# A blocked triangular inverse inside an RWKV-7 scan: rank-1 updates kept to 16x16 diagonal blocks, the block below them by fp32 products on TensorE

## The chip, the cores and the metric

The kernel runs on one core of one Trainium2 chip. The metric is device time in microseconds (us) of one execution. The engines are called as the profile calls them: PE (TensorE, matrix products; PEld is its weight load), DVE (VectorE), ACT (ScalarE), POOL (GpSimd) and SP (SyncE, which issues the DMAs).

## The reference, cut to what matters

Two groups of 512 tokens go through two layers: RWKV-7 time mixing (layer 0) and neighbourhood attention (layer 1). The change touches layer 0 alone, where for 16 heads of width 64, in both directions, this recurrence is computed:

```python
def step(s, inp):
    r_t, w_t, k_t, v_t, a_t, b_t = inp
    sa = jnp.einsum('bhvk,bhk->bhv', s, a_t)
    s = s * w_t[:, :, None, :] + sa[..., None] * b_t[:, :, None, :] + v_t[..., None] * k_t[:, :, None, :]
    return s, jnp.einsum('bhvk,bhk->bhv', s, r_t)
```

## The kernel before

**Chunks.** The scan is worked in chunks of 64 tokens, eight for each sequence. Inside a chunk the terms `sa` of the 64 tokens depend on each other through a strictly lower triangular matrix of scalar products ("gram"), so each chunk needs the inverse of a unit triangular 64x64 matrix for each head and direction. The work goes in eight sets: two sequences `s`, and for each four pairs of head pairs `pb`. A set has 4 heads, 2 directions and 8 chunks, which makes 64 matrices of 64x64; they lie in two halves of the partitions as 32 units.

**Stages of a set.** `prep` (called twice for a set by `preps`) builds decays and the four scaled operands `ab`, and `gram` multiplies them (L951) and copies the 32x32 diagonal blocks into `Gd` (L957) and the blocks below them into `Go` (L958). `inverse` turns these into `MT`, the transposed inverses. Then eight `step`s run, one for each chunk and direction pair: each solves with `MT` (L1189), forms outputs (L1213) and the next state `S` (L1209, L1221, L1223). `finish` normalises what the eight steps left.

**The inverse.** For each of 128 partitions, `N` holds one 32x32 diagonal block in its rows, so that 128 blocks are worked at once. Thirty rank-1 updates, each a product (L994) and a sum (L996) over the rows below, invert the block. A mask (L998) and a diagonal of ones (L1000) follow, then two transposes of 32x32 blocks (L1004 into `NA`, L1009 into `MT`). ACT and POOL spread `MT` (L1013, L1014), and PE multiplies twice with 32x32 tiles (L1025, L1027) to get the block below the two diagonal blocks of the 64x64 matrix, with copies by ACT in between (L1032, L1035).

**What else runs in the same phase.** The dense products of the layer ("columns") run in the background: 80 columns of 128 outputs, each 8 trios of 128x128 by 128x512 products in a split fp32 form (L802, L803, L804), 640 trios in all. Their weights are split into a high and a low part by ACT (L721) and DVE (L723), their inputs likewise (L747, L749).

**What sets the order.** All of this is written as threads (`step`, `alone`, `near`, `outer`, `preps`, `inverse`, `finish`, the parts of `flow`), and `weave` decides at build time, with the estimated durations in `Clock`, in which order their pieces are put on PE, DVE and ACT. The order on the chip is fixed: each engine takes its instructions one after the other, and one that waits holds up all behind it. A thread has a rank; `step` has 0, `preps` 1.5, `inverse` 5, the columns 9, and lower goes first. Where nothing can run on PE for a while in its estimates, `weave` puts in filler products whose results nobody reads (L1622). `MT` has two buffers, so the inverse of a set waits for the steps of the set two before it. `Gd` has one buffer, so the second half of the gate in `preps` (`did["gd"] >= n`) holds back the preparation of a set until the inverse before it has taken its copy.

```python
yield "S", lambda: did["gd"] >= n and did["inverse"] >= n - 1      # preps
yield "D", lambda: did["preps"] > n and did["steps"] >= NCH * (n - 1)   # inverse
Thread(lambda: 5, inverse()), Thread(lambda: 1.5, preps())
```

After the scan phase `rest` runs the remaining columns of layer 0, and layer 1.

## Time and profile before

| | |
|---|---|
| median of 3 runs | 1686.07 us (1684.14 to 1687.42) |
| the profiled execution | 1683.88 us, of it the span of the trace 1682.1 us |
| mean granted TensorE clock | 0.971 of full speed |
| busy, share of the span: PE, PEld, DVE, ACT, POOL | 93%, 71%, 73%, 58%, 1% |
| first solve of the eight steps of a set (L1189), us from the start | 321, 443, 558, 664, 790, 920, 1041, 1115 |
| last step of the scan (L1213) | 1162 |
| last trio of the background columns in this phase | 1179 |

The profile is of one execution. All times in it count from the start of the span. A row of the timeline has a start, a duration, the engine, the line and the operation, with output and inputs by the program's names; rows of a table by stretch have the stretch, its length, and for each engine the busy time and the number of instructions in it. An fp32 product has two records in the trace, so 512 products of a line show as x1024.

### The profile page before, as it was taken

What the parts mean: (1) busy time and instruction counts of PE and PEld (TensorE: products, weight loads), DVE (VectorE), ACT (ScalarE), POOL (GpSimd) and SP (SyncE); (2) the same over time, 40 slices, a digit from 0 to 9 for tenths busy, and PEclk for the clock granted to TensorE, in tenths of its full rate; (3) what the DMA queues carried; (4) which work ended last, traced back from release to release, by engine and by line L of the source; (5) the groups of instructions that cost most, each with busy time, mean ns of one, the idle gap of its engine ahead of it and who ended that gap; (6) DMA issues with size and microseconds to landing.
All of it is one profiled execution on the core that took longest, in us unless ns stands there. A gap on an engine that the chain in (4) does not pass through costs nothing.

```text
span 1682.1 us, 46291 instructions
## 1 busy us (share of the span) xinstructions
PE 1570.9 (93%) x18818; PEld 1201.2 (71%) x18818; DVE 1227.8 (73%) x2725; ACT 984.0 (58%) x1977; POOL 24.1 (1%) x94
## 2 busy tenths in 40 slices
PE   7989898899989998989998999999999899999998
PEld 6767666676766776767765767777777687777776
DVE  8985668688777697887888887865576856555564
ACT  5443655676655667755674665454577655555562
POOL 0000000000000000000000000000000000000000
PEclk9989999899999999999997999999999999999999
DMA  5435678678586786876776665554774347555553
GB/s 209 163 125 187 203 243 261 202 228 257 170 262 211 225 255 205 259 243 205 241 232 214 202 199 199 184 178 131 267 231 155 111 127 249 182 157 175 164 181 107
DMA packets 240821, 336.26 MB, mean 200 GB/s; under 512 B 53696, under 2 KB 119360, under 8 KB 240608
## 3 DMA queue, kind: packets, MB, share of 16 engines
q1 hardware_dynamic: 240608, 333.31, 61.6%
q8 instruction: 148, 2.42, 0.6%
q14 instruction: 65, 0.53, 0.1%
HBM read 227.71 MB, written 105.51 MB: 198 GB/s over the span
## 4 chain that ended last, share of the span: by engine, by line
PE 67%; DVE 11%; DMA 9%; ACT 8%; issue 4%; SPq 1%; DVEq 0%; POOL 0%; ACTq 0%; POOLq 0%
PE pm L802 7%; PE pg L423 6%; PE pg L424 6%; PE pg L425 6%; PE pm L804 5%; PE pm L803 5%; PE pf L1090 2%; PE sc L1433 2%; PE us L1209 2%; DMA cab<-dab 2%; PE po L1466 2%; PE pt L1451 2%; PE zy L1162 2%; PE us L1189 2%; PE zy L1213 1%
## 5 line engine op out<-in xcount | busy, mean ns | idle before, releaser
L802 PE MATMUL pm<-act,whi 128*128 128x512 f32 x640 | 287.6, 449 | 16.1 <-ACT act L771 7.2
L804 PE MATMUL pm<-act,wlo 128*128 128x512 f32 x640 | 256.7, 401 | 12.2 <-DVE wlo L723 12.2
L803 PE MATMUL pm<-act,whi 128*128 128x512 f32 x640 | 258.0, 403 | 5.1 <-DVE act L749 4.2
L423 PE MATMUL pg<-act,whi 128*128 128x512 f32 x448 | 182.4, 408 | 5.9 <-ACT act L372 5.5
L424 PE MATMUL pg<-act,whi 128*128 128x512 f32 x448 | 178.1, 398 | 0.1
L425 PE MATMUL pg<-act,wlo 128*128 128x512 f32 x448 | 177.5, 396 | 0.0
L802 PEld LDWEIGHTS pm<-act,whi 128*128 128x128 f32 x640 | 122.6, 192 | 63.8 <-issue 16.1
L372 ACT CAST whi<-raw 128x512 fp32r<-128x512 f32 x148 | 91.4, 619 | 129.3 <-PE pg L424 75.3
L804 PEld LDWEIGHTS pm<-act,wlo 128*128 128x128 f32 x640 | 123.4, 193 | 44.3 <-DVE wlo L723 16.9
L373 DVE TENSOR_TENSOR wlo<-raw,whi 128x512 fp32r<-128x512 f32 x148 | 101.4, 687 | 70.2 <-ACT whi L372 63.0
L803 PEld LDWEIGHTS pm<-act,whi 128*128 128x128 f32 x640 | 123.6, 193 | 29.6 <-DVE act L749 7.2
L723 DVE TENSOR_TENSOR wlo<-raw,whi 128x512 fp32r<-128x512 f32 x160 | 108.7, 684 | 42.9 <-ACT whi L721 39.5
L721 ACT CAST whi<-raw 128x512 fp32r<-128x512 f32 x160 | 98.1, 616 | 51.7 <-PE pm L803 14.5
L423 PEld LDWEIGHTS pg<-act,whi 128*128 128x128 f32 x448 | 84.8, 190 | 24.8 <-ACT act L372 6.1
L425 PEld LDWEIGHTS pg<-act,wlo 128*128 128x128 f32 x448 | 84.8, 189 | 17.9 <-issue 0.8
L424 PEld LDWEIGHTS pg<-act,whi 128*128 128x128 f32 x448 | 84.9, 190 | 17.4 <-issue 2.0
L996 DVE TENSOR_TENSOR N<-etmp,N 128x30 f32<-128x30 f32 (+14 forms) x240 | 78.5, 327 | 4.2
L994 DVE TENSOR_TENSOR etmp<-N 128x30 f32<-128x30 f32 (+14 forms) x240 | 78.3, 326 | 4.2
L1444 DVE CUSTOM_DVE_ANT_0 sb<-sc,bias 128x256 f32<-128x256 f32 x128 | 49.2, 419 | 31.1 <-PE pt L1451 23.5
L1090 PE MATMUL pf<-cab 64*64 64x128 f32 (+1 forms) x2048 | 67.9, 268 | 2.2 <-issue 2.1
L1447 ACT ACTIVATE sb<-sb,mx 128x256 f32<-128x256 f32 x128 | 63.9, 504 | 9.1 <-DVE mx L1446 9.0
L1113 DVE TENSOR_TENSOR AK<-zy,cc 128x256 f32<-128x256 f32 x63 | 26.6, 421 | 53.5 <-PE zy L1068 51.6
(389 smaller groups left out, 3389.7 us busy)
## 6 DMA issues: line engine op xcount, KB each, us to landing
dab<-ab SPq DMA_DIRECT2D x32, 1024.0 KB, 5.5
cab<-dab SPq DMA_DIRECT2D x64, 512.0 KB, 4.4
raw<-in_w_in_dram SPq DMA_DIRECT2D x128, 256.0 KB, 3.3
bias<-in_rpb_dram SPq DMA_DIRECT2D x32, 384.0 KB, 4.8
raw<-in_w_z_dram SPq DMA_DIRECT2D x32, 256.0 KB, 4.5
dz<-tmp SPq DMA_DIRECT2D x32, 256.0 KB, 3.0
raw<-in_w_k_dram SPq DMA_DIRECT2D x32, 256.0 KB, 4.0
dk<-tmp SPq DMA_DIRECT2D x32, 256.0 KB, 2.2
```

Source lines behind the costliest of these rows:

```text
L372: self.nc.scalar.copy(hi, src)
L373: (eng or self.nc.vector).tensor_tensor(lo, src, hi.bitcast(F32), op=ALU.subtract)
L423: nc.tensor.matmul(ps, hi, x[k][0], start=(k == 0), stop=False)
L424: nc.tensor.matmul(ps, hi, x[k][1], start=False, stop=False)
L425: nc.tensor.matmul(ps, lo, x[k][0], start=False, stop=(k == KT - 1))
L721: nc.scalar.copy(hi, raw[h])
L723: nc.vector.tensor_tensor(lo, raw.pop(h), hi.bitcast(F32), op=ALU.subtract)
L802: nc.tensor.matmul(ps, hi[:, at], xh, start=(k == 0), stop=False)
L803: nc.tensor.matmul(ps, hi[:, at], xl, start=False, stop=False)
L804: nc.tensor.matmul(ps, lo[:, at], xh, start=False, stop=(k == KT - 1))
L996: vt.tensor_tensor(N[:, q + 1:, :q], tv, N[:, q + 1:, :q], op=ALU.add)
L1090: end = nc.tensor.matmul(st.f[half(a), h, 0, d, g] if st.last else st.f[half(a), h, :, d, g], ab[half(h), d, g, 2 * e[d] + 1 - a], rt if s ...
```

## The change

The rank-1 updates now work only inside the two 16x16 blocks on the diagonal of each 32x32 block: 14 updates instead of 30, with both 16x16 blocks in one instruction (a leading dimension of 2 in the access pattern `blocks`). The two 16x16 blocks off the diagonal of `N` are zeroed by a memset on POOL. The mask covers 512 elements in place of 1024. Both transposes now write into `MT`, and the tile `NA` is gone; `N` is used again in its place.

The 16x16 block below the two diagonal blocks is then made by three rounds of fp32 products on PE (`each`): 32 units, four positions of the PE array (rows and columns 0, 32, 64, 96), 128 products of 32x32 by 32x16 in a round, all into one PSUM tile. Between the rounds DVE evacuates once (a scaling by a 0/1 column and an added identity) and ACT twice. A round waits for the evacuation before it. What follows, the 64x64 step with L1025 and L1027, stays, reading `MT` and `N` in place of `NA`.

`Gd` gets a second buffer, and the gate `did["gd"] >= n` is dropped from `preps`. Two small constants are made once at the start. Line numbers behind the change are higher by 3 to 29.

```diff
+        self.i32 = cp.tile([P, 33], F32, tag="i32", name="i32")
+        nc.vector.tensor_reduce(self.i32[:, 0:32], self.ident.rearrange("p (q m) -> p m q", q=4), axis=AX.X, op=ALU.add)
+        nc.vector.tensor_reduce(self.i32[:, 32:33], self.i32[:, 16:32], axis=AX.X, op=ALU.add)
...
-                self.t("wc", (P, 2, 2, NCH), 4, F32, self.front), self.t("Gd", (P, 2, NCH, 2, 32), 1, F32, self.front),
+                self.t("wc", (P, 2, 2, NCH), 4, F32, self.front), self.t("Gd", (P, 2, NCH, 2, 32), 2, F32, self.front),
...
-        tmp = f("etmp", (P, 256))
-        self.did["gd"] += 1
-        for q in range(1, 31):
-            n = 31 - q
-            tv = tmp[:, :n * q].rearrange("p (i j) -> p i j", i=n)
+        tmp = f("etmp", (P, 128))
+
+        def blocks(o, i, j):
+            x = N[:, 0, 0:1]
+            return bass.AP(tensor=x.tensor, offset=x.offset + o, ap=[list(x.ap[0]), [16 * 33, 2], list(i), list(j)])
+
+        x = N[:, 0, 16:17]
+        gps.memset(bass.AP(tensor=x.tensor, offset=x.offset, ap=[list(x.ap[0]), [16 * 31, 2], [32, 16], [1, 16]]), 0.0)
+        for q in range(1, 15):
+            n = 15 - q
+            tv = tmp[:, :2 * n * q].rearrange("p (b i j) -> p b i j", b=2, i=n)
+            here = blocks(32 * (q + 1), (32, n), (1, q))
             yield "D"
-            vt.tensor_tensor(tv, N[:, q + 1:, q:q + 1].broadcast_to([P, n, q]), N[:, q:q + 1, :q].broadcast_to([P, n, q]), op=ALU.mult)
+            vt.tensor_tensor(tv, blocks(32 * (q + 1) + q, (32, n), (0, q)), blocks(32 * q, (0, n), (1, q)), op=ALU.mult)
             yield "D"
-            vt.tensor_tensor(N[:, q + 1:, :q], tv, N[:, q + 1:, :q], op=ALU.add)
+            vt.tensor_tensor(here, tv, here, op=ALU.add)
         yield "D"
-        vt.tensor_tensor(N, N, self.lower, op=ALU.mult)
+        here = blocks(0, (32, 16), (1, 16))
+        vt.tensor_tensor(here, here, self.lower[:, 0:16, 0:16].unsqueeze(1).broadcast_to([P, 2, 16, 16]), op=ALU.mult)
...
-        NA = f("NA", (P, NU, 32))
-        vt.transpose(NA.rearrange("p u j -> p j u"), N.rearrange("p i j -> p j i"))
+        vt.transpose(MT[:, :, 1, :].rearrange("p u j -> p j u"), N.rearrange("p i j -> p j i"))
         yield "D"
         vt.transpose(MT[:, :, 0, :].rearrange("p u i -> p i u"), N)
         yield "A"
+        act.copy(N[:, :, 16:32], self.i32[:, 16:32].unsqueeze(1).broadcast_to([P, NU, 16]))
+        quarters = [slice(32 * q, 32 * q + 32) for q in range(4)]
+
+        def each(lhs, rhs, *xs):
+            yield "P", free, lambda c: max(room(c), need(*xs)(c))
+            ps = self.p("pm", (P, NU, 16))
+            for u in range(NU):
+                for q in quarters:
+                    nc.tensor.matmul(ps[q, u], lhs(q, u), rhs(q, u), start=True, stop=True, tile_position=(q.start, q.start))
+            return ps
+
+        ps = yield from each(lambda q, u: gd[q, u], lambda q, u: MT[q, u, 1, 0:16], MT, Gd)
+        yield "D", None, need(ps)
+        vt.scalar_tensor_tensor(
+            N[:, :, 0:16], ps, self.i32[:, 32:33], self.i32[:, 0:16].unsqueeze(1).broadcast_to([P, NU, 16]), op0=ALU.mult, op1=ALU.add)
+        ps = yield from each(lambda q, u: MT[q, u, 0], lambda q, u: N[q, u, 0:16], MT, N)
+        yield "A", None, need(ps)
+        act.copy(MT[:, :, 1, 0:16], ps)
+        ps = yield from each(lambda q, u: N[q, u], lambda q, u: MT[q, u, 0, 16:32], MT, N)
+        yield "A", None, need(ps)
+        act.copy(MT[:, :, 0, 16:32], ps)
+        yield "A"
...
-                            nc.tensor.matmul(ps[y, j], go[x, u], NA[x, u], start=True, stop=True, tile_position=(64 * h, 64 * h + 32))
+                            nc.tensor.matmul(ps[y, j], go[x, u], MT[x, u, 1], start=True, stop=True, tile_position=(64 * h, 64 * h + 32))
...
-                yield "S", lambda: did["gd"] >= n and did["inverse"] >= n - 1
+                yield "S", lambda: did["inverse"] >= n - 1
```

**What moves on PE.** Of the 640 trios of the columns, those that stand ahead of the first solve of the last set are 596 before and 428 now; the rest, 44 before and 212 now, stand behind it. The filler products (L1622) are 97 before and 70 now. On PE, around the products of the second set's inverse, before (names ending in numbers are buffers; "x31" stands for 31 more of the same):

```order
L802 MATMUL pm_5001<-act_4070,whi_4940 128x512
L803 MATMUL pm_5001<-act_4069,whi_4940 128x512
L804 MATMUL pm_5001<-act_4070,wlo_4941 128x512
L1025 MATMUL pm_5030<-NA_4982,Go_2466 32x32 [waits DVE_49,Activation_49]
L1025 MATMUL pm_5030<-NA_4982,Go_2466 32x32 x31
L802 MATMUL pm_5001<-act_4113,whi_4970 128x512
```

and the rounds of the same inverse in the change (the first and the second, with what stands between them):

```order
L1028 MATMUL pm_4474<-MT_440_1700,Gd_2468 32x16 x128
L1191 MATMUL zy_4627<-S_4470,cab_441_1701 64x64 [waits DVE_49]
L1191 MATMUL zy_4627<-S_4470,cab_441_1701 64x64 x15
L1197 MATMUL zy_4627<-V_4239,AK_4439 64x64 [waits DMAHW5_49]
L1197 MATMUL zy_4627<-V_4239,AK_4439 64x64 x7
L954 MATMUL pf_4656<-ab_4211 32x64 [waits Activation_49]
L954 MATMUL pf_4656<-ab_4211 32x64 x31
L683 MATMUL pm_4691<-cc,tmp_4383 128x128 x4
L1028 MATMUL pm_4701<-N_3818,MT_440_1700 32x16 [waits DVE_49]
L1028 MATMUL pm_4701<-N_3818,MT_440_1700 32x16 x63
```

Before, trios of columns stand on both sides of the inverse's products; in the change, products of a step (L1191, L1197) and of a gram (L954) of the sets around it stand between two rounds.

On DVE, the end of the second set's updates in the change (L1250 and L1252 make the state of a step of the first set, L1142 and L1152 its factors):

```order
L1004 TENSOR_TENSOR etmp_3820<-N_3818 128x28 [waits DVE_49]
L1152 TENSOR_TENSOR R_4314<-pf_4285,mrx_1696 128x512 [waits PE_49]
L919 TENSOR_TENSOR ab_4211<-kp_873_4306,u_4208 128x4x2x64 [waits DVE_49]
L1250 TENSOR_TENSOR S_4334<-us_4268,S_4180 128x256 [waits PE_49,Activation_49]
L1006 TENSOR_TENSOR N_3818<-etmp_3820,N_3818 128x2x14 [waits DVE_49]
L1252 TENSOR_TENSOR S_4334<-S_4334,wc_1785 128x256 [waits DVE_49]
L1259 TENSOR_TENSOR y_3124<-zy_4214,y_3124 128x256 [waits PE_49]
L1009 TENSOR_TENSOR N_3818<-N_3818,cc 128x2x16x16 [waits DVE_49]
L1011 MEMSET N_3818 128x32 [waits DVE_49,Pool_49]
```

Before, the last update of the second set stands behind the last step of the first set and its `finish`; in the change it stands among the steps of the first set, as the states `S` show.

More of the change, by code (lines that the diff above doesn't have):

```diff
@@ L987, in inverse @@
         vt.transpose(N, gd.rearrange("p u t -> p t u"))
-        tmp = f("etmp", (P, 256))
-        self.did["gd"] += 1
-        for q in range(1, 31):
-            n = 31 - q
-            tv = tmp[:, :n * q].rearrange("p (i j) -> p i j", i=n)
+        tmp = f("etmp", (P, 128))
[8 more added lines that the diff above has]
+            here = blocks(32 * (q + 1), (32, n), (1, q))
             yield "D"
-            vt.tensor_tensor(tv, N[:, q + 1:, q:q + 1].broadcast_to([P, n, q]), N[:, q:q + 1, :q].broadcast_to([P, n, q]), op=ALU.mult)
+            vt.tensor_tensor(tv, blocks(32 * (q + 1) + q, (32, n), (0, q)), blocks(32 * q, (0, n), (1, q)), op=ALU.mult)
             yield "D"
-            vt.tensor_tensor(N[:, q + 1:, :q], tv, N[:, q + 1:, :q], op=ALU.add)
+            vt.tensor_tensor(here, tv, here, op=ALU.add)
         yield "D"
-        vt.tensor_tensor(N, N, self.lower, op=ALU.mult)
+        here = blocks(0, (32, 16), (1, 16))
+        vt.tensor_tensor(here, here, self.lower[:, 0:16, 0:16].unsqueeze(1).broadcast_to([P, 2, 16, 16]), op=ALU.mult)
         yield "D"
         vt.memset(N.rearrange("p i j -> p (i j)")[:, 0:1024:33], 1.0)
-        yield "D"
-        NA = f("NA", (P, NU, 32))
-        vt.transpose(NA.rearrange("p u j -> p j u"), N.rearrange("p i j -> p j i"))
         MT = self.MTb[self.nM % 2]
@@ L1008, in inverse @@
         yield "D"
+        vt.transpose(MT[:, :, 1, :].rearrange("p u j -> p j u"), N.rearrange("p i j -> p j i"))
+        yield "D"
         vt.transpose(MT[:, :, 0, :].rearrange("p u i -> p i u"), N)
         yield "A"
+        act.copy(N[:, :, 16:32], self.i32[:, 16:32].unsqueeze(1).broadcast_to([P, NU, 16]))
[18 more added lines that the diff above has]
+        yield "A"
         for q in (1, 3):
-            r = slice(32 * q, 32 * q + 32)
+            r = quarters[q]
             act.copy(MT[r, :, 1], MT[r, :, 0])
@@ L1017, in inverse @@
                 us = slice(j0, j0 + 16)
-                yield "P", free, (lambda c: max(room(c), need(NA)(c))) if step == 0 else (lambda c: max(room(c), need(MT)(c)))
+                yield "P", free, lambda c: max(room(c), need(MT, N)(c))
                 ps = self.p("pm", (P, 16, 32))
@@ L1021, in inverse @@
                     for h in range(2):
-                        x, y = slice(64 * h, 64 * h + 32), slice(64 * h + 32, 64 * h + 64)
+                        x, y = quarters[2 * h], quarters[2 * h + 1]
                         u = j0 + j
                         if step == 0:
-                            nc.tensor.matmul(ps[y, j], go[x, u], NA[x, u], start=True, stop=True, tile_position=(64 * h, 64 * h + 32))
+                            nc.tensor.matmul(ps[y, j], go[x, u], MT[x, u, 1], start=True, stop=True, tile_position=(64 * h, 64 * h + 32))
                         else:
-                            nc.tensor.matmul(ps[x, j], NA[y, u], MT[y, u, 1], start=True, stop=True, tile_position=(64 * h + 32, 64 * h))
+                            nc.tensor.matmul(ps[x, j], N[y, u], MT[y, u, 1], start=True, stop=True, tile_position=(64 * h + 32, 64 * h))
                 yield "A", None, need(ps)
@@ L1030, in inverse @@
                     if step == 0:
-                        y = slice(64 * h + 32, 64 * h + 64)
-                        act.copy(NA[y, us], ps[y])
-                    else:
-                        x = slice(64 * h, 64 * h + 32)
-                        act.copy(MT[x, us, 1], ps[x])
+                        act.copy(N[quarters[2 * h + 1], us], ps[quarters[2 * h + 1]])
+                    else:
+                        act.copy(MT[quarters[2 * h], us, 1], ps[quarters[2 * h]])
         self.formed[s, pb] = wc, MT
```

## The prediction

> **What bounds the kernel now.** First I read the table by stretch, cut at the first solve of the first set (321 us), of the seventh (1041) and near the end of the scan.

> ```profile
> core 0: us, PE busy (x) PEld busy (x) DVE busy (x) ACT busy (x) POOL busy (x), PEclk, DMA share, GB/s
> 0.00:321.00 321.00, 284.61 (x1873) 215.36 (x1873) 245.48 (x449) 177.35 (x321) 8.26 (x57) 0.96 0.59 197
> ...
> 790.00:920.00 130.00, 118.02 (x1935) 88.93 (x1938) 112.52 (x216) 82.24 (x157) 2.35 (x6) 0.92 0.71 231
> ...
> 321.00:1041.00 720.00, 664.77 (x11501) 499.39 (x11499) 578.56 (x1122) 458.38 (x894) 14.00 (x35) 0.96 0.71 225
> 1041.00:1200.00 159.00, 157.88 (x2798) 120.83 (x2795) 101.79 (x204) 73.87 (x139) 1.89 (x2) 1.00 0.54 179
> ```

> TensorE is busy for 665 of the 720 us in the middle (92%), VectorE for 579 (80%, and 87% in the worst stretch), ScalarE for 64%. Behind 1041 us TensorE is at 99% and its clock at 1.00; in the middle it idles for 55 us at a clock of 0.96. So the kernel is near a TensorE bound, and what can still be won lies in those 55 us, the clock and the filler products.

> Second, the timeline around the second inverse shows who waits for it.

> ```profile
> 330.64 0.18 DVE L994 TENSOR_TENSOR etmp<-N 128x30 f32<-128x30 f32 x1
> ...
> 381.61 0.69 PE L1213 MATMUL zy<-X,R 128*64 128x64 f32 x16
> ...
> 422.52 0.19 DVE L996 TENSOR_TENSOR N<-etmp,N 128x30 f32<-128x30 f32 x1
> ...
> 428.63 0.39 PE L802 MATMUL pm<-act,whi 128*128 128x512 f32 x1
> 428.86 0.39 PE L803 MATMUL pm<-act,whi 128*128 128x512 f32 x1
> 429.08 0.39 PE L804 MATMUL pm<-act,wlo 128*128 128x512 f32 x1
> 429.40 1.20 PE L1025 MATMUL pm<-NA,Go 32*32 32x32 f32 x64
> 430.53 0.50 PE L802 MATMUL pm<-act,whi 128*128 128x512 f32 x1
> ...
> 440.32 1.20 PE L1027 MATMUL pm<-MT,NA 32*32 32x32 f32 x64
> ...
> 443.04 0.27 PE L1189 MATMUL us<-Z,MT 64*64 64x64 f32 x1
> ```

> The sixty updates last from 330.6 to 422.7 us, 92 us, though they hold VectorE for about 20: with rank 5 they go between everything else. The first set's last step is over at 382 us, and the second set's first solve starts at 443. Such a gap lies between all sets. It is no idle time, though: the trios of the columns fill it (428.6 to 429.4, and again behind 430.5). That is why a shorter chain need not shorten the run.

> Third, who ends the waits of TensorE in the middle (first number: us in all):

> ```profile
> PE pm L804 <- DVE wlo L723: 8.5, 4, 3.5
> PE pm L802 <- ACT act L771: 7.2, 4, 4.0
> PE pm L1285 <- DVE bv L1279: 5.9, 2, 5.1
> PE us L1209 <- ACT X L1201: 4.6, 6, 2.1
> ```

> The largest are for VectorE's and ScalarE's preparations; none is for the inverse itself.

> **The change, part by part.** VectorE first.

> ```profile
> L996 DVE TENSOR_TENSOR N<-etmp,N 128x30 f32<-128x30 f32 (+14 forms) x240 | 78.5, 327 | 4.2
> L994 DVE TENSOR_TENSOR etmp<-N 128x30 f32<-128x30 f32 (+14 forms) x240 | 78.3, 326 | 4.2
> ...
> L994 DVE TENSOR_TENSOR etmp<-N 128x108 f32<-128x108 f32 x16 | 4.3, 267 | 0.3
> ...
> L994 DVE TENSOR_TENSOR etmp<-N 128x58 f32<-128x58 f32 x16 | 3.4, 214 | 0.2
> ...
> L994 DVE TENSOR_TENSOR etmp<-N 128x30 f32<-128x30 f32 x16 | 3.1, 194 | 0.4
> ...
> L998 DVE TENSOR_TENSOR N<-N,cc 128x1024 f32<-128x1024 f32 x8 | 9.8, 1222 | 0.2
> ...
> L1288 DVE SCALAR_TENSOR_TENSOR bv<-pm,dv,bv 128x512 f32<-128x512 f32 x16 | 11.9, 745 | 1.2 <-PE pm L1285 0.7
> ...
> L723 DVE TENSOR_TENSOR wlo<-raw,whi 128x512 fp32r<-128x512 f32 x160 | 108.7, 684 | 42.9 <-ACT whi L721 39.5
> ```

> Removed are 60 instructions an inverse, (78.5 + 78.3) / 8 = 19.6 us. The 28 new ones have 28 to 112 elements; between the rows of 30 (194 ns), 58 (214) and 108 (267) they come to 1.67 us for seven sizes, twice up and down, twice for product and sum: 6.7 us. The mask falls from 1222 ns to the 684 of 512 elements; the evacuation from PSUM adds 745. In all 12.7 us less an inverse, 102 us in eight. VectorE is not the bound, so this counts only as far as TensorE waits for it. ScalarE gets three copies of 512 elements an inverse, which at the 586 ns of the row below is 14 us in eight, in its 36% of free time: nothing. POOL's memset stands many updates ahead of the one instruction that needs it (L1011), and POOL is busy for 14 of 720 us: nothing; were it stuck behind another POOL wait, the mask and the transposes would be late, which is part of the second rival.

> ```profile
> L683 ACT COPY vs<-pm x32: 561/586/604, 271.8 to 706.4; 128x512 f32<-128x512 f32 x32
> ...
> L1025 PE MATMUL pm<-NA,Go x1024: 184/191/213, 300.7 to 1108.0; 32*32 32x32 f32 x171
> ...
> 311.99 1.92 PE L1027 MATMUL pm<-MT,NA 32*32 32x32 f32 x64
> ...
> 407.14 0.86 PE L951 MATMUL pf<-ab 64*32 64x64 f32 x64
> ...
> 391.61 1.02 PE L1622 MATMUL zy<-cc 128*128 128x256 f32 x4
> ```

> TensorE's added work is 24 rounds of 128 products. No row shows four positions with 16 columns. The nearest is L1025: 32 products (64 records) at two positions in 1.20 us less the last record's own 0.19, 32 ns each. L951, on tiles of 64x32, takes (0.86 - 0.2) / 32 = 21 ns. If a product holds its position for as long as at L1025, 64 ns, four positions give 16 ns; that is my value, 2.05 us a round. It lies between 8 ns, if half the columns also halve the time, and 54 ns, the slow L1027 above ((1.92 - 0.19) / 32), if nothing overlaps. Going to small tiles and back costs 0.2 us (from 429.08 to 430.53 are 1.45 us, less 1.01 of work and 0.23 for the trio's last). So 24 x 2.25 = **54 us**, between 29 and 171.

> [...]

> The filler products fall from 97 to 70: four take 1.02 us, (1.02 - 0.38) / 3 = 213 ns a record and 0.43 us each, so 27 give back **12 us**. The 168 trios that move behind the scan cost the same there as before, 0.23 us a product: no gain, no loss, and they are why the shorter chain isn't gained as such.

> The wait between the sets goes. What is late next is TensorE itself. In the 159 us behind 1041, where trios and steps fill it, it idles for 1 us. With VectorE relieved by 13 us in each set and the inverse done among the steps of the set before, I take the middle's idle share from 55/720 = 7.7% to 2.5% of some 650 us, 16 us: **39 us** less, 0 to 55 being possible. Half of the lost clock (0.96 to 0.98 in 650 us) is **14 us**, 0 to 28. The second buffer for `Gd` and the looser gate are within these; alone they move a preparation ahead, which costs nothing while VectorE has 20% free.

> Sum: 54 - 12 - 39 - 14 = -11 us on the span of 1682.1, so 1671; with the 1.8 us around the span 1673. The median of the runs is 2.2 us above the profiled execution (1686.07 to 1683.88), so **1675 us** is forecast.

> **The rivals.** *TensorE's idle time stays.* Nothing in the list of waits names the inverse; steps wait for ScalarE's copies and columns for split weights as before, and ahead of the scan's end there are fewer trios to fill with. Then 54 - 12 = 42 us are added: 1728. It decides from the point where idle and clock give back less than 42 us. For it speaks the filled gap in the timeline; against it, that VectorE at 80 to 87% is what the waits for L723 and L1279 stand behind.

> *The rounds wait.* The second round stands behind the first with only a few step and gram products between them and waits for VectorE's evacuation, the third for ScalarE's; behind the waiting product stand the next step's solve and its factors. Sixteen such returns at 1.8 us (evacuation 0.75, and as much again until VectorE is free, plus the 0.2 of a product's end) are 28 us: 1703. Against it: L1191, L1197 and L954 stand in between and fill most.

> *All of it is gained.* If VectorE's load was what held TensorE, the whole 55 us and 28 of clock go: 54 - 12 - 83 = -41, so 1645. For it speaks 790 to 920 us, where VectorE is at 87% and the clock at 0.92.

> *The positions don't overlap.* Then the rounds cost 171 us and not 54; 1675 + 117 = 1792 at most. Against it speaks L1025.

> That the change doesn't do what it says is no case of its own: the order shows the updates among the first set's steps.

> **How the numbers follow.** Chances: forecast 0.47 (its own range 1655 to 1690), idle stays 0.22, rounds wait 0.13, all gained 0.13, no overlap 0.05. The range for 8 in 10 goes from a little below all gained to short of the first rival's end, 1640 to 1725; left out are no overlap, about half of the first rival and the far end of all gained. A measurement of this kernel tells about 0.2% (3.4 us) from no change. Faster: 0.13 of all gained and 0.37 of the forecast, 0.50. Within 0.2%: 0.07 of the forecast and 0.02 of the rounds' waits, 0.09. Slower: 0.03 of the forecast, 0.11, 0.22 and 0.05 of the others, 0.41.

> **What would show it.** In the profile after: the updates' line with 28 instructions a set and about 6.5 us; L1028 with 6144 records and 2.0 us a round (4 us or more: the third part of my sum is wrong); first solves of the sets 60 to 100 us apart in place of 74 to 130, the last one 100 us or more earlier, and a longer stretch of trios alone at the end. Right, if TensorE's idle time before the last set's first solve is near 16 us and its clock near 0.98; wrong, if the idle time is 40 or more, whichever instruction then waits. If waits of the second and third rounds lead the list, the second rival has it.

## The result, and the profile after

| | before | after |
|---|---|---|
| median | 1685.11 us (1682.66 to 1687.42, 4 runs) | 1864.41 us (1858.63 to 1870.13, 4 runs) |
| ratio, 95% interval | 1 | 1.1072 (1.1042 to 1.1101) |
| span and mean granted TensorE clock of the profiled execution | 1682.1 us, 0.971 | 1863.1 us, 0.925 |
| first solve of the eight steps of a set, us (now L1218) | as above | 332, 450, 564, 645, 837, 958, 1069, 1151 |
| last trio of the background columns | as above | 1355 |

The change makes the kernel 179 us slower. I had forecast 1675 us, with 1725 as the upper end.

First the table by stretch of the kernel after, cut at the first solve of the first, the seventh and the last set and near the last trio (columns as in the prediction).

```profile
332.00:1069.00 737.00, 626.81 (x15603) 478.12 (x15599) 460.21 (x834) 417.02 (x827) 17.25 (x42) 0.88 0.62 193
1069.00:1151.00 82.00, 69.70 (x2221) 56.06 (x2214) 35.53 (x81) 33.17 (x65) 2.42 (x3) 0.83 0.37 118
1151.00:1380.00 229.00, 221.95 (x1929) 175.75 (x1919) 128.47 (x258) 105.98 (x195) 0.00 (x0) 0.99 0.59 192
```

In the middle TensorE now idles for 737 - 627 = 110 us where it idled for 55, and its clock is 0.88 instead of 0.96. VectorE is down to 62% there. The long dense stretch of trios behind the last set is there as the order said, but the last set's first solve is later than before, not 100 us earlier.

Second, who ends the waits (the whole execution, first number us in all):

```profile
PEld pm L1028 <- issue: 86.7, 51, 4.8
...
PE pm L1028 <- issue: 77.6, 38, 4.7
...
ACT MT L1037 <- PE pm L1028: 48.4, 7, 14.3
...
ACT MT L1040 <- PE pm L1028: 35.5, 7, 7.8
```

TensorE's largest waits are in front of the new products, and what ends them is called "issue": time in which the engine waits for nothing that the profile shows, neither a semaphore nor data. PE and PEld are two records of the same TensorE, so its idle time there is the 77.6 us of PE, and the 86.7 of PEld are mostly the same pauses seen a second time. ScalarE waits for the rounds, not the rounds for ScalarE. The view of line L1028 alone adds the two up:

```profile
L1028 PE MATMUL pm<-N,MT x2048: 172/209/232, 288.7 to 1112.5; 32*32 32x16 f32 x187
...
  issue: 164.4, 89
```

Third, the timeline of TensorE around the second and third round of the third inverse shows where these waits stand:

```profile
514.92 1.90 PE L1028 MATMUL pm<-N,MT 32*32 32x16 f32 x128 [1.43 <-issue]
518.65 1.41 PE L1028 MATMUL pm<-N,MT 32*32 32x16 f32 x89 [1.83 <-issue]
519.99 1.12 PE L1242 MATMUL zy<-X,R 128*64 128x64 f32 x16
...
524.94 1.35 PE L1028 MATMUL pm<-MT,N 32*32 32x16 f32 x85
526.48 1.90 PE L1028 MATMUL pm<-MT,N 32*32 32x16 f32 x128 [0.18 <-issue]
530.49 0.82 PE L1028 MATMUL pm<-MT,N 32*32 32x16 f32 x43 [2.12 <-issue]
```

The pauses are in the middle of a round, between products that depend on nothing new, and the pieces between two pauses hold 128 records (a whole round is 256: 85, 128 and 43 in the second one shown). Each record has a weight load beside it (the page has x24908 of both), so a piece is 256 instructions. From 514.92 to 518.65 such a piece takes 3.73 us, from 526.48 to 530.49 4.01 us, though its records run for 1.9 us, at a granted clock of 0.50. The list of DMA queues has the same step of 256: before

```profile
q8 instruction: 148, 2.42, 0.6%
```

and after

```profile
q8 instruction: 195, 3.19, 0.7%
```

These are packets and MB. The 6144 new records with their 6144 loads are 12288 instructions, and 12288 / 47 more packets = 261 instructions a packet. Worked out from the records of L1028, the 24 rounds last 4.0 to 8.3 us each from the first start to the last, 152 us in all; I had booked 2.05 us. This gave the theory that the runs test: **TensorE's instructions come in blocks of 256, one in some 3.4 to 4 us (the 3.73 and 4.01 above, and 3.44 between two packets that start at 512.52 and 515.96 us), so a burst of 512 short instructions takes up to 7 or 8 us whatever its products need.**

VectorE's part came out as forecast:

```profile
L1006 DVE TENSOR_TENSOR N<-etmp,N 128x28 f32<-128x28 f32 (+6 forms) x112 | 26.9, 240 | 2.3
...
L1004 DVE TENSOR_TENSOR etmp<-N 128x28 f32<-128x28 f32 (+6 forms) x112 | 26.8, 239 | 2.2
...
L1033 DVE SCALAR_TENSOR_TENSOR N<-pm,i 128x512 f32<-128x512 f32 x8 | 6.0, 746 | 9.7 <-PE pm L1028 9.7
L1009 DVE TENSOR_TENSOR N<-N,cc 128x512 f32<-128x512 f32 x8 | 5.5, 687 | 0.1
```

Updates (26.9 + 26.8) / 8 = 6.7 us an inverse, mask 687 ns, evacuation 746 ns: near the three values of the prediction.

### The profile page after: what moved, and what is told of

Same layout as the page of the kernel before. It is cut to its first block, busy times and chain, and to the rows that moved or that the text cites. A ratio compares the mean times of both kernels' runs of the same rounds, so it can differ in the third digit from the quotient of the medians.

```text
span 1863.1 us, 58356 instructions
## 1 busy us (share of the span) xinstructions
PE 1665.4 (89%) x24908; PEld 1291.7 (69%) x24908; DVE 1149.7 (62%) x2479; ACT 996.9 (54%) x1997; POOL 28.3 (2%) x102
## 4 chain that ended last, share of the span: by engine, by line
PE 70%; DMA 8%; issue 8%; DVE 7%; ACT 6%; SPq 0%; DVEq 0%; ACTq 0%; POOL 0%; POOLq 0%
PE pm L805 8%; PE pm L806 6%; PE pm L807 6%; PE pg L426 5%; PE pg L427 5%; PE pg L428 5%; PE pm L1028 4%; PE pf L1119 3%; PE sc L1462 2%; DMA cab<-dab 2%; PE us L1238 2%; PE zy L1191 2%; PE po L1495 2%; PE us L1218 2%; PE zy L1242 1%
## 5 line engine op out<-in xcount | busy, mean ns | idle before, releaser
L426 PE MATMUL pg<-act,whi 128*128 128x512 f32 x448 | 185.5, 415 | 3.1 <-ACT os L1519 1.9
L427 PE MATMUL pg<-act,whi 128*128 128x512 f32 x448 | 179.2, 400 | 4.8 <-DVE act L376 4.8
L805 PEld LDWEIGHTS pm<-act,whi 128*128 128x128 f32 x640 | 126.1, 197 | 53.5 <-issue 8.6
L806 PEld LDWEIGHTS pm<-act,whi 128*128 128x128 f32 x640 | 126.6, 198 | 31.7 <-DVE act L752 6.6
L1142 DVE TENSOR_TENSOR AK<-zy,cc 128x256 f32<-128x256 f32 x63 | 26.5, 421 | 103.4 <-PE zy L1097 101.4
L1119 PE MATMUL pf<-cab 64*64 64x128 f32 (+1 forms) x2048 | 73.6, 279 | 3.5 <-issue 2.3
L1230 ACT COPY X<-us 64x256 f32<-64x256 f32 x128 | 46.8, 366 | 35.8 <-PE zy L1097 31.8
L1119 PEld LDWEIGHTS pf<-cab 64*64 64x64 f32 x2048 | 60.0, 143 | 4.8 <-issue 4.3
```

The lines of the kernel that those rows point to most:

```text
L426: nc.tensor.matmul(ps, hi, x[k][0], start=(k == 0), stop=False)
L427: nc.tensor.matmul(ps, hi, x[k][1], start=False, stop=False)
L805: nc.tensor.matmul(ps, hi[:, at], xh, start=(k == 0), stop=False)
L806: nc.tensor.matmul(ps, hi[:, at], xl, start=False, stop=False)
L1119: end = nc.tensor.matmul(st.f[half(a), h, 0, d, g] if st.last else st.f[half(a), h, :, d, g], ab[half(h), d, g, 2 * e[d] + 1 - a], rt if s ...
```

## The experiments

Ratios are to the kernel before on the same chip. "Packets" are those of the instruction queue as above. Line numbers are those of each run's own kernel.

### The rounds: instructions or products?

**after_wide** keeps each round's columns but not its instructions.

```diff
-            for u in range(NU):
-                for q in quarters:
-                    nc.tensor.matmul(ps[q, u], lhs(q, u), rhs(q, u), start=True, stop=True, tile_position=(q.start, q.start))
+            a, b = [lhs(q, 0) for q in quarters], [rhs(q, slice(0, NU)) for q in quarters]
+            for q in range(4):
+                nc.tensor.matmul(ps[quarters[q]], a[q], b[q], start=True, stop=True, tile_position=(32 * q, 32 * q))
```

(The planner still books a round as 128 products, which keeps the order.)

> The change, with each round's 128 products of 32x32 by 32x16 replaced by four products of 32x32 by 32x512, one for each position, into the same tile; order, evacuations and waits stay, the instructions of a round fall from 512 to 16. It leaves out the weights of 31 of 32 units, so the lower blocks aren't the reference's. Theory (TensorE's instructions come in at no more than one block of 256 in about 3.4 us, so a round of 512 takes 6.9 us whatever its products need): a round falls to between 0.9 us (two of the filler's 0.43 us products' columns, four positions at once) and 3.4 us (one position after the other), so 24 rounds give back 84 to 144 us, and the clock some 30 more: 1690 to 1760. Rival 1 (the returns over VectorE and ScalarE and the new order are what costs): nothing of that is changed, 1840 to 1870. Rival 2 (products of four positions into one bank go one by one): the round still takes 3.4 us, and the time falls by no more than 80.

Measured: 1738.23 us, ratio 1.0323 (1.0287 to 1.0360), 149 packets. 126 us of the loss are gone with order, columns and waits as they were; what fell is the number of products and weight loads, and with it that of the instructions, from 512 to 16 a round. The line of the rounds, first start to last start, shows how long a product of 512 columns takes (min/median/max ns, then first and last start):

```profile
L1037 PE MATMUL pm<-N,MT x64: 584/612/1057, 279.4 to 997.3; 32*32 32x512 f32 x64
```

From the first to the last start of a round's eight records of 0.6 us pass 0.47 to 0.50 us in 19 of the 24 rounds and 0.87 in the other five (from the records): four positions into one tile overlap. Rival 1 (returns and order) and rival 2 (one position after the other) are out as the main cause. What returns cost when the rounds are short, the waits of this run show:

```profile
PE pm L1037 <- DVE N L1044: 15.4, 5, 6.5
```

**after_no_rounds** removes the three calls of `each` and the three evacuations.

> The change without its three rounds and their three evacuations; the 16x16 blocks below the diagonal blocks are left out. It shows what the 28 updates, the second buffer for the grams and the looser gate bring by themselves. Theory: everything above 1685 comes from the rounds, so the time is below the kernel before: 1620 to 1675 (my prediction less its 54 us is 1621). Rival (the shorter chain and the moved trios are themselves the loss): 1690 or more.

Measured: 1697.67 us, ratio 1.0084 (1.0049 to 1.0119), 148 packets. So the rounds cost 1864.4 - 1697.7 = **167 us**, and the rest of the change isn't a gain: it is 14 us slower than before, where I had 1621. My theory's range is missed, the rival's is met; the second group of runs is about this.

The 167 us aren't pauses alone. The row of engines on the page of the change (the row of this run stands further down, at after_spaced):

```profile
PE 1665.4 (89%) x24908; PEld 1291.7 (69%) x24908; DVE 1149.7 (62%) x2479; ACT 996.9 (54%) x1997; POOL 28.3 (2%) x102
```

So with the rounds TensorE is idle for 71 us more and busy for 96 us more. At 16 ns each the products are 49 of the 96. Most of the rest is the clock, by an estimate: its records hold only the values 1.00 and 0.50, TensorE is busy at 0.50 for 205 us in the change and for 98 us here, and half of the difference is 54 us.

**before_burst** puts the rounds into the kernel before, with no result that anyone needs.

```diff
+    def idle(self, units):
+        for u in range(units):
+            for q in range(0, P, 32):
+                self.nc.tensor.matmul(
+                    self.spare[q:q + 32, 16 * (u % 16):16 * (u % 16) + 16], self.ident[q:q + 32, q:q + 32], self.scan[0][q:q + 32, 0:16],
...
+                if (step, j0) != (1, 16):
+                    self.idle(32)
                 ps = self.p("pm", (P, 16, 32))
```

> The kernel before, order unchanged, with 24 rounds of 128 products of 32x32 by 32x16 at four positions added, three in each inverse ahead of three of the four groups of 32 products of the 64x64 step. They read constants and their output is read by nobody, so that nothing waits for a result. Theory (instruction supply): 6.9 us a round, 166 us, less what hides in TensorE's idle time, more for a lower clock: 1790 to 1870. Rival (a round costs what its products take, 2.25 us, and the rest of the change's loss comes from waits for results): 54 us at most, 1700 to 1740.

Measured: 1874.32 us, ratio 1.1144 (1.1092 to 1.1196), 196 packets. 190 us are lost though nothing waits for the products; the range I gave is just exceeded. The timeline around one of the bursts (L978) shows that the pause can also fall on the instructions behind the burst:

```profile
588.20 1.34 PE L978 MATMUL zy<-cc 32*32 32x16 f32 x138
589.71 1.18 PE L978 MATMUL zy<-cc 32*32 32x16 f32 x118 [0.17 <-issue]
590.76 0.31 PE L1035 MATMUL pm<-NA,Go 32*32 32x32 f32 x9
593.54 1.35 PE L1035 MATMUL pm<-NA,Go 32*32 32x32 f32 x55 [2.47 <-issue]
...
595.42 0.63 PE L803 MATMUL pm<-act,whi 128*128 128x512 f32 x1
595.85 0.63 PE L804 MATMUL pm<-act,wlo 128*128 128x512 f32 x1
```

The 256 records run in 2.6 us here, at a clock of 1.00 and nearer to the 2.05 that I had booked; why they are faster behind these trios was not shown. The pause comes behind them, 2.5 us in the middle of L1035, whose products are as they were.

**before_pieces** spreads the same products.

```diff
+            if did["k"] % 6 == 0 and self.gone < did["k"] <= 576:
+                self.gone = did["k"]
+                self.idle(8)
```

> The kernel before, order unchanged, with the same 3072 idle products as in 24 rounds, but in 96 pieces of 32 products, each behind every sixth trio of the columns. Theory: 6 trios of 0.7 us and a piece hold 36 + 128 instructions, fewer than 256 in 3.4 us, so the supply keeps up and a piece costs 0.5 us for its products and 0.2 for the change of tile size: 68 us, less what hides in idle time: 1720 to 1760. Rival (every product costs the same wherever it stands): the same as in the burst.

Measured: 1759.24 us, ratio 1.0449 (1.0413 to 1.0485), 196 packets. As many products and packets as the burst, 115 us less. A piece in the timeline:

```profile
644.92 0.39 PE L804 MATMUL pm<-act,wlo 128*128 128x512 f32 x1
645.24 0.73 PE L978 MATMUL zy<-cc 32*32 32x16 f32 x64
645.90 0.50 PE L802 MATMUL pm<-act,whi 128*128 128x512 f32 x1
```

0.73 us less the last record's own 0.18 is 0.55 us for 32 products, 17 ns each. I had taken 16: the price of a product was right where its instructions are there. 96 pieces lose 75 us, 0.78 each: 0.55 for the products, and the 0.23 left over is what going to small tiles and back comes to. TensorE's idle time is that of the kernel before (110.7 us to 111.1), though pauses are not quite gone: its waits put down to "issue" are 30 us in all, where the burst has 87 and the kernel before 7.

**before_burst_half** uses 16-bit operands in the bursts, so that a product is one load and one matmul (L978 has x3072 of each, and x6144 in the burst).

```diff
-                    self.spare[q:q + 32, 16 * (u % 16):16 * (u % 16) + 16], self.ident[q:q + 32, q:q + 32], self.scan[0][q:q + 32, 0:16],
+                    self.spare[q:q + 32, 16 * (u % 16):16 * (u % 16) + 16], self.ident[q:q + 32, q:q + 16].bitcast(mybir.dt.bfloat16), self.scan[0][q:q + 32, 0:8].bitcast(mybir.dt.bfloat16),
```

> The burst of idle products again (24 rounds of 128 at the same places of the kernel before, same order), but of 16-bit operands, so that a product is one weight load and one matmul in place of two of each: 256 instructions a round in place of 512. Theory (the cost goes by instructions: the burst's 190 us over 24 rounds of 512 are 15.5 ns each): half of it, 1684 + 95 = 1779, between 1755 and 1800. Rival (the cost goes by products or by changes of tile size): as much as the burst, 1850 to 1875.

Measured: 1766.45 us, ratio 1.0467 (1.0432 to 1.0502), 172 packets. Half the instructions lose 82 of 190 us. By itself this doesn't part instructions from products, because the time that TensorE is busy with the idle products also falls, from 73 to 30 us; but its waits put down to "issue" halve as well, from 87 to 41 us. Per packet that comes on top, the burst loses 190 / 48 = 4.0 us, the half burst 82 / 24 = 3.4, the rounds of the change 167 / 47 = 3.5, and the spread pieces 75 / 48 = 1.6.

The records show the block itself. I count the records of PE and PEld together, those of semaphores included, in order of start from the first of the execution, in blocks of 256. All waits of PE over 1 us that are put down to "issue", 38 in the change and 38 in before_burst, then end on the 194th or 195th record of a block, and so do the five over 0.4 us in the kernel before. Each of the 76 also ends 1.2 to 1.6 us after a packet of the instruction queue has landed. For three pauses of the change shown above, the packets start at 512.52, 515.96 and 527.77 us and land at 513.43, 517.16 and 529.06; the pauses end at 514.92, 518.65 and 530.49, and the next packet starts about 1.1 us behind that. So what TensorE waits for there is its next block of instructions.

**after_pieces** should mend the change by issuing a round in four pieces.

```diff
+                    yield "P", None, lambda c, at=self.clock.pe() + 1500.0: at
+                for u in range(u0, u0 + 8):
```

> The change with each round of 128 products issued as four pieces of 32 products, the planner holding the next piece back by 1.5 us of its own estimate so that trios or steps go between; nothing is left out. Theory (instruction supply): a piece of 32 takes 0.55 us as it did for the idle pieces in the kernel before, where 96 pieces added 75 us; on the 1698 us of the change without rounds that makes 1773, between 1750 and 1795. Rival (what the rounds cost is the wait for their results and the place where they stand): the chain of the inverse is longer still, 1860 or more.

Measured: 1856.26 us, ratio 1.1009 (1.0971 to 1.1046). A miss: the theory's 1773 isn't met. The timeline tells why:

```profile
777.23 1.01 PE L1034 MATMUL pm<-MT,N 32*32 32x16 f32 x98
780.86 1.26 PE L1034 MATMUL pm<-MT,N 32*32 32x16 f32 x128 [2.62 <-issue]
784.60 0.61 PE L1034 MATMUL pm<-MT,N 32*32 32x16 f32 x30 [2.48 <-issue]
```

Nothing stands between the pieces of this round; the planner found no trio to put there, and on the chip the pieces ran together. No trio stands in any of the 72 gaps between pieces: 23 are empty, the others hold other products. The pauses stand at 128 records as before. From 780.86 to 784.60 are 3.74 us, the step of 514.92 to 518.65 in the change (3.73), though the 128 records run for 1.26 us here, at a clock of 1.00, and for 1.90 there, at 0.50. So the step doesn't come from how fast the products run. The edit hadn't done what it was meant to do, so the next one forces trios between the pieces.

**after_spaced** (the edit is shown against after_pieces)

```diff
-                    yield "P", None, lambda c, at=self.clock.pe() + 1500.0: at
+                    yield "P", None, lambda c, at=self.clock.pe(), k=self.did["k"]: at + (0.0 if self.did["k"] >= k + 3 else 8000.0)
```

> The change with each round in four pieces of 32 products, where the next piece waits in the planner until three trios of the columns have been put behind the last one (or 8 us of its estimate have gone); nothing is left out. In the pieces before (1856 us) most gaps held no trio at all, but products of steps and grams, which are as dense in instructions, or nothing, so the whole stretch of a round still took 3.2 to 4.6 us for 256 instructions. Theory (instruction supply): three trios are 18 instructions in 2.1 us, so piece and gap hold 146 in 2.6 us, slower than the supply, and a piece costs what it did among the columns of the kernel before (75 us for 96): 1698 + 75 = 1773, between 1745 and 1800. Rival (what a round costs in the change isn't the supply but its place in the chain of the inverse): the chain gets longer, 1850 or more.

Measured: 1811.02 us, ratio 1.0775 (1.0751 to 1.0799). 53 us come back, with every product and packet of the change still there, but 38 fewer than expected, and outside the range of the theory. The busy rows of the page, first without rounds and then spaced, split the difference:

```profile
PE 1569.2 (93%) x18806; PEld 1205.5 (71%) x18806; DVE 1140.7 (67%) x2471; ACT 991.2 (58%) x1985; POOL 28.4 (2%) x102
```

```profile
PE 1649.7 (91%) x24856; PEld 1254.7 (69%) x24856; DVE 1151.8 (64%) x2479; ACT 1003.1 (55%) x2003; POOL 28.4 (2%) x102
```

TensorE's busy time is 80 us longer, near the 75 of the spread pieces. The other 32 of the 112 us between the spans (1695.6 and 1807.9) are idle time. Its waits between 300 and 1300 us begin with

```profile
PE pm L1320 <- DVE bv L1314: 19.0, 7, 4.2
PE pm L805 <- DVE bv L1314: 7.4, 3, 3.3
PE pm L1034 <- issue: 6.5, 5, 2.7
```

The pauses ahead of the new products, 77.6 us in the change, are down to 6.5; a wait for one VectorE instruction leads in their place. So it is the supply that gave the 53 us back; that the 80 us are the products and their changes of tile size is read from the 75 of before_pieces, not shown by itself. How much of the 32 us is the new order and how much the longer chain wasn't tried.

### The rest of the change: why was there no gain?

**before_no_updates** drops all rank-1 updates.

```diff
-        for q in range(1, 31):
-            n = 31 - q
...
-            vt.tensor_tensor(N[:, q + 1:, :q], tv, N[:, q + 1:, :q], op=ALU.add)
```

> The kernel before with all thirty rank-1 updates of each inverse left out (480 VectorE instructions, 157 us of its busy time), everything else as it was. It bounds what any shorter chain of updates can bring. Theory A (TensorE is the bound and VectorE's updates lie beside it): 1670 to 1700. Theory B (VectorE's load is what TensorE waits for): 1630 or less.

Measured: 1684.45 us, ratio 1.0006 (0.9985 to 1.0027). The page rows of before and of this kernel:

```profile
PE 1570.9 (93%) x18818; PEld 1201.2 (71%) x18818; DVE 1227.8 (73%) x2725; ACT 984.0 (58%) x1977; POOL 24.1 (1%) x94
```

```profile
PE 1556.6 (93%) x18758; PEld 1196.3 (71%) x18758; DVE 1099.0 (65%) x2245; ACT 986.8 (59%) x1977; POOL 24.2 (1%) x94
```

VectorE works 129 us less and the time doesn't move. Leaving out the whole chain of updates, which the change halves, brings nothing with the order that the planner chooses for it.

**gate_only** (two buffers, looser gate, merged transposes, old updates, no rounds) and **gate_back** (the same with one buffer and the old gate):

```diff
-                yield "S", lambda: did["inverse"] >= n - 1
+                yield "S", lambda: did["gd"] >= n and did["inverse"] >= n - 1
```

> The kernel before with the second buffer for the grams, the looser gate and the transposes written without their own tile, as in the change; the 30 updates over 32x32 blocks stay and there are no rounds, so the result is the reference's. The change without rounds took 1698 us, 14 more than before, where I had booked some 60 less. Theory A (VectorE's relief is worth nothing because TensorE's idle time isn't due to it, and the earlier preparations are neutral): within 10 us of 1698, or between it and 1684. Theory B (the relief is worth the 40 to 50 us I booked, and the looser gate takes as much away by moving preparations into the steps): 1730 or more.

> The kernel before with 30 updates over 32x32 blocks, no rounds, one buffer for the grams and the old gate; of the change only the two transposes into one tile and the constants are left. With the second buffer and the looser gate it took 1714 us. Theory A (the looser gate costs these 30 us): 1678 to 1692. Theory B (the missing tile of the transposes does): 1705 to 1720.

Measured: 1714.46 us, ratio 1.0176 (1.0146 to 1.0206), and 1709.40 us, ratio 1.0166 (1.0145 to 1.0186). The first lies between the two theories' values, 16 above the one and 16 below the other. The second settles the gate: it is neutral, and what is left, the merged transposes with the constants, comes to 28 us. **no_rounds_gate** says the same of the change without rounds:

> The change without its rounds (the lower 16x16 blocks left out), and with one buffer for the grams and the old gate, so that of the change only the 28 updates are left. Theory A (the looser gate costs here what it cost with the old updates): 1698 - 30 = 1668, between 1660 and 1684. Theory B (TensorE's work sets the time, 480 updates less brought nothing, and the gate's 30 us were an order that doesn't carry over): 1684 to 1700.

Measured: 1697.16 us, ratio 1.0094 (1.0060 to 1.0128). With the looser gate it was 1697.67; theory A falls.

The last four runs part the updates, the merged tile and the order. A recorded order takes the place of the planner in three of them:

```diff
-            for t in ts:
...
-            t.step()
+        for j, n in ORDER:
...
+                    threads[j].step()
```

**updates_only** and **updates_replay** have the 28 updates alone (with their smaller mask and the memset), the first with an order that the planner chooses, the second with the order of before.

> The kernel before with the 28 updates in 16x16 blocks in place of the 60 (the lower 16x16 blocks are left out), its own tile for the transposes, one buffer for the grams, the old gate, no rounds; the planner is free to choose its order. Theory A (VectorE's relief brings nothing, and the 13 us of the change without rounds come from the merged tile): 1675 to 1690. Theory B (the relief brings nothing and any new order costs some 15 us): 1692 to 1710. Theory C (the relief is worth 15 us or more and the merged tile ate it): 1670 or less.

> The same 28 updates in the kernel before, but with every other instruction in exactly the order of the kernel before, so that the only difference is that VectorE has 32 instructions fewer in each of eight inverses (some 100 us of its busy time in all). Theory (TensorE sets the time; VectorE's updates fill gaps of its own): 1678 to 1688. Rival (TensorE waits for VectorE's load): 1665 or less.

Measured: 1690.42 us, ratio 1.0033 (1.0017 to 1.0049), and 1679.97 us, ratio 0.9965 (0.9950 to 0.9980). The first lies between the ranges of its theories A and B, the second meets its theory. In a fixed order 256 VectorE instructions fewer are worth 5 us. The table by stretch, before and then with the 28 updates, both from the first set's first solve to the last set's:

```profile
321.00:1115.00 794.00, 738.33 (x13033) 555.02 (x13035) 635.69 (x1248) 494.74 (x963) 15.89 (x37) 0.96 0.70 220
```

```profile
321.00:1109.00 788.00, 728.76 (x13011) 548.95 (x13012) 557.28 (x1024) 494.28 (x963) 19.60 (x44) 0.98 0.70 222
```

VectorE falls from 80% to 71% of the stretch, and TensorE's idle time stays: 56 us, then 59. So VectorE's load wasn't what it waited for.

**merged_replay** has the merged transposes in the order of before, **before_replay** the kernel before in the order that the planner chooses for the merged transposes.

> The kernel before with both transposes written into one tile, as in the change, and every instruction in exactly the order of the kernel before. With the order that the planner chose for it (and two small constants) it took 1709 us. Theory A (the waits on the shared tile cost the 25 us): 1700 to 1715. Theory B (the order does): 1680 to 1690.

> The kernel before, nothing changed but the order of its instructions, which is the one that the planner chose for the merged tile. Theory A (the waits on the shared tile cost the 25 us): 1680 to 1690. Theory B (the order does): 1700 to 1715.

Measured: 1691.18 us, ratio 1.0045 (1.0028 to 1.0062), and 1717.73 us, ratio 1.0181 (1.0151 to 1.0211). Both lie 1 to 3 us above the range of theory B and farther from that of theory A. The shared tile costs 6 us, the order 33; the two don't simply add, since gate_back, which has both, loses 28. Part of the order's cost can be named, the filler products, before and then in the other order:

```profile
L1622 PE MATMUL zy<-cc 128*128 128x256 f32 x194 | 51.1, 401 | 0.0
```

```profile
L1673 PE MATMUL zy<-cc 128*128 128x256 f32 x260 | 71.8, 415 | 0.0
```

33 more products of 0.43 us are 14 us, and the busy time of the two rows differs by 20.7. How much of that would have been idle time without them wasn't tried. No run points to a version that beats the kernel before by more than the 5 us of updates_replay, which leaves the lower blocks out.

## Why the prediction was wrong, point by point

- **The bound.** "Near a TensorE bound": right, and shown by before_no_updates. I didn't draw the consequence: what the middle could win was then not VectorE's to give.
- **VectorE's relief, 12.7 us an inverse.** Right in size by the rows (on the page, where overlapping records count once, VectorE's busy time falls by 78 us and not by 102). Worth 5 us in all in a fixed order (updates_replay).
- **The added products, 54 us: the step that failed.** I priced a product by the hold of a tile position in a burst of 32, "16 ns; that is my value, 2.05 us a round", and the bounds of 29 and 171 us both came from how positions overlap. The 16 ns were right where the instructions are there and the clock is full (17 in before_pieces); in the change's own rounds TensorE is busy for 79 us, 26 ns a product, with the clock at 0.50 for 46 of them and about 0.2 us more at the end of each piece. What I left out is where 512 instructions come from. The kernel before has few bursts long enough to show it; two rows of its waits did, both on the 194th or 195th record of a block, and I passed over them as small:

```profile
PE zy L1068 <- issue: 2.7, 1, 2.7
...
PE pf L1090 <- issue: 2.1, 1, 2.1
```

  The row of 148 packets was on its page too. Measured: 167 us, 3.4 to 4.0 us a block in each of the bursts, in place of 54. The upper bound of 171 lay close by coincidence, and I gave it 0.05.
- **Idle time 55 to 16 us and the clock, 39 + 14 us: the second step that failed.** Measured without the rounds: nothing of it. Between the first set's first solve and the last set's, TensorE idles for 70 us at a clock of 0.95:

```profile
298.00:1023.00 725.00, 654.93 (x12713) 493.20 (x12713) 534.14 (x986) 478.65 (x940) 19.81 (x46) 0.95 0.73 229
```

  I read VectorE's 80 to 87% as the cause of TensorE's idle time because the two stood in the same stretch; the list of waits that I quoted named 26 us in four rows for several engines and none for the updates. The rival "TensorE's idle time stays" was right in its mechanism for this part, and its price of 42 us was too small mainly because it took over the 54: with 167 it is 155, of the 179 measured.
- **Filler products, 12 us.** 97 to 70 in the change, as the order showed. The order also costs and gives in other places: the change without its rounds is 14 us slower than before, while the updates in a fixed order are 5 us faster.
- **Trios behind the scan, ScalarE's copies, POOL's memset, gate and second buffer: nothing.** Right for the gate (gate_back, no_rounds_gate). That the merged transposes cost nothing was assumed without a price; they cost 6 us, and 33 by the order that they lead to.
- **Rounds wait for returns (1703).** Not the cause: before_burst loses as much with no returns at all. In after_wide, where the rounds are short, TensorE waits 15.4 us for the first return in all, about half of the 28 that I had given the rival.
- **Positions don't overlap (1792).** Wrong mechanism: 17 ns a product at four positions into one tile (before_pieces), where the rival had 54 ns; and in after_wide eight records of 0.6 us, at four positions into one tile, start within 0.47 to 0.87 us.
- **The test I had named** ("4 us or more: the third part of my sum is wrong") picked out the right step.

## What to carry to other kernels

Count instructions as well as time: if a burst is short in microseconds but long in instructions, divide it by the block that the instruction queue's row gives (261 instructions a packet here) and compare with what other work stands around it; where other, long instructions stand between, the same products cost less than half (75 us in before_pieces, 190 in before_burst). An engine that is 87% busy beside one that is 92% busy needn't be the cause of the other's idle time: leave its work out, in a fixed order, before pricing its relief. Where a planner sets the order, a change that does nothing can cost 30 us through the order alone (33 in before_replay), so compare in a recorded order.
